# Mixture-of-experts kernel on one core: TensorE's order written out, and three groups of transfers moved to another queue

## The chip, the core and the metric

The kernel runs on one core of a Trainium2 chip. The metric is the device time of one execution in microseconds; lower is better. The engines are named as in the profile: PE (TensorE), DVE (VectorE), ACT (ScalarE), POOL (GpSimd) and SP (SyncE, which here only issues transfers). Each of these engines runs its own instructions in a fixed order, and an instruction that waits holds up all behind it on its engine.

## What is computed

Two transformer blocks are applied to 256 tokens of width 1024, in float32. The first block has attention, then a mixture of experts, then a gated side input; the second has attention beside a gated recurrence, then a feed-forward part. The change touches only the mixture of experts:

```python
logits = xt @ w_router + b_router            # 256 tokens, 32 experts
top_logit, top_e = top_k(logits, 4)
gate = softmax(top_logit)
# for each expert e and the tokens xs that chose it
hh = xs @ w_gu[e] + b_gu[e]                  # 1024 -> 2048
glu, lin = split(hh)
act = min(glu, 7) * sigmoid(1.702 * min(glu, 7)) * (clip(lin, -7, 7) + 1)
y = act @ w_dn[e] + b_dn[e]                  # 1024 -> 1024
out[token] += gate * y
```

## The kernel before

All weights are read once from HBM. Each expert has 12 MiB of them: four chunks of 2 MiB of `w_gu`, keys `("gu", e, 0..3)`, and two chunks of 2 MiB of `w_dn`, keys `("dn", e, 0..1)`. A list `plan` holds all chunks in the order in which they are wanted: for each e the four gu chunks of expert e and then the two dn chunks of expert e-1. `load_next(ring)` takes the next entry of the plan and starts its transfer into a buffer of one of four rings (a: 3 buffers, b: 5, c: 1, d: 1, the last until expert 10 alone). `done(key)` is called behind the last matmul on a chunk and starts the next chunk into the freed buffer, so a transfer waits until PE has finished with the buffer. Ring a takes none of the last six expert chunks; it is kept for `("pg", 0)`, `("pg", 1)` and `("in2", 0)`, the first weights of the next stage. The chunk `("R",)`, a table for the second block, comes in between at expert 16.

Nearly all chunks are issued by SP. Two of the last four, `("dn", 30, 1)` and `("dn", 31, 0)`, are issued by POOL, and the last, `("dn", 31, 1)`, is issued by SP in two halves.

At most 64 tokens of an expert are handled by the main loop. The steps for one expert, with their names and lines:

- `slots(e)`: DVE builds two one-hot matrices from the token positions, `oh` and `gg`.
- `gather(e)` (L949 to L961): 48 small bf16 matmuls pick the expert's tokens into `xg` (PSUM), which DVE multiplies into SBUF; then two transposes and four tiny matmuls turn `gg` and the gates into the tile `y`, which DVE copies into `gt` and `gs`.
- `up(e)` (L973): 64 matmuls on the four gu chunks; two ACTIVATEs evict the result into `h1`.
- `glu(e)` (L988): eight transposes of `h1`, then the clamped activation on DVE and ACT, giving `gl`.
- `down_part(e, c)` (L1009): 16 matmuls on a dn chunk, twice; then ACT and DVE evict `y` into a high part (`li`) and a low part (`sg`).
- `scatter(e)` (L1037): 16 matmuls spread the rows of `y` over the tokens, and DVE adds them onto `h`.

The order of the calls in the loop is that in the diff below. It is not the order on the engines: a scheduler of the language, working from its own estimates, orders each engine's instructions, and `tc.issue_after` ties some of them. With `tc.manual_schedule(engines={PE})` PE's instructions keep the order in which the program calls them, and the other engines stay with the scheduler.

Tokens past an expert's 64 are handled by `past_slots()`, once, at expert 14. It is a branch on the largest count (`tc.If`, L1075 and L1076), with loops, matmuls and transfers in it. The inputs do not take it, but every engine has to pass it.

The functions with their lines:

Of the kernel before, what the change touches and what calls it, by code (L numbers as in the profile page):

```python
# [25 lines left out]
FT = mybir.dt.float32  # L26
# [5 lines left out]
OP = mybir.AluOpType  # L32
# [4 lines left out]
P = 128  # L37
S = 256
D = 1024
E = 32  # L40
# [64 lines left out]
def block_kernel(ctx: ExitStack, tc: tile.TileContext, A, out, dbg=None, parts=("t1", "moe", "over", "t3")):  # L105
    nc = tc.nc
    V, SC, PE, G, SY = nc.vector, nc.scalar, nc.tensor, nc.gpsimd, nc.sync
# [15 lines left out]
    def tt(o, a, b, op):  # L123
        return V.tensor_tensor(out=o, in0=a, in1=b, op=op)  # L124
# [20 lines left out]
    xn = keep.tile([P, 2, D], FT, name="h")  # L145
# [37 lines left out]
    wg, wd = A["w_gu"], A["w_dn"]  # L183
# [27 lines left out]
    def load_next(ring):  # L211
        i = state["next"]
        if i >= len(plan) or (ring != "a" and i >= stop_moe) or (ring == "d" and not state["d"]):
            return
        if ring == "a" and stop_moe - 6 <= i < stop_moe:

            state["held"] += 1
            return
        state["next"] = i + 1
        key, ap, shape = plan[i]  # L220
        t = rings[ring].tile([P, 4096], FT, name="w")
        n = int(np.prod(shape[1:]))
        v = t[:, :n]
        if len(ap.shape) == 3:
            v = v.rearrange("p (a b) -> p a b", b=ap.shape[2])
        if i == 0:
            for h in range(2):
                SY.dma_start(v[:, h], ap[:, h])
        elif key in (("dn", E - 2, 1), ("dn", E - 1, 0)):
            G.dma_start(v, ap)  # L230
        elif key == ("dn", E - 1, 1):
            for h in range(2):
                SY.dma_start(v[:, 2 * h:2 * h + 2], ap[:, 2 * h:2 * h + 2])
        else:
            SY.dma_start(v, ap)
        if key == ("R",):
            SY.dma_start(t[0:E, 3072:3072 + D], A["b_dn"])
        live[key] = (t, ring)
        if i + 1 == stop_moe:
            for _ in range(state["held"]):  # L240
                load_next("a")
# [648 lines left out]
    sl_ = {}  # L890
# [49 lines left out]
    xgs, GTs, GSs, ysb = {}, {}, {}, {}  # L940

    def gather(e):
        oh, gg = sl_.pop(e)
        px = px_.tile([P, 8, CAP], FT, name="xg")
        for kd in range(8):
            n = 0
            for t in range(2):
                for i in range(3):
                    PE.matmul(px[:, kd], u3[i][:, t, kd * P:(kd + 1) * P], oh[:, t], start=(n == 0), stop=(n == 5))  # L949
                    n += 1  # L950
        xg = mw.tile([P, 8, CAP], FT, name="xg", bufs=1)
        tt(xg, px, vec[:, VCOL["g_moe"]:VCOL["g_moe"] + 8].unsqueeze(2).to_broadcast([P, 8, CAP]), OP.mult)
        pgt = py_.tile([P, 512], FT, name="y")
        for t in range(2):
            PE.transpose(pgt[:, t * P:(t + 1) * P], gg[:, t], ident)
        for t in range(2):
            PE.matmul(pgt[:, S:S + 2], gg[:, t], gtab[:, t, e], start=(t == 0), stop=(t == 1))
        gt = mw.tile([P, S], FR, name="gt", bufs=3)
        V.tensor_copy(gt, pgt[:, 0:S])
        gs = mw.tile([P, 2], FT, name="gs", bufs=3)  # L960
        V.tensor_copy(gs, pgt[:, S:S + 2])  # L961
        xgs[e], GTs[e], GSs[e] = xg, gt, gs

    def up(e, aside=None):
        xg = xgs.pop(e)
        ps = pg_.tile([P, 2, 512], FT, name="gu")
        for c in range(4):
            w = W(("gu", e, c)).rearrange("p (k n) -> p k n", k=2)
            for kk in range(2):
                k = 2 * c + kk  # L970
                for n in range(2):
                    for s in range(2):
                        PE.matmul(ps[64 * s:64 * s + 64, n], xg[:, k],  # L973
                                  w[:, kk, s * 1024 + n * 512:s * 1024 + (n + 1) * 512],
                                  start=(k == 0), stop=(k == 7))
            done(("gu", e, c))
            if aside and c == 0:
                aside()
        h1 = mw.tile([P, 2, 512], FT, name="h1", bufs=1)
        for n in range(2):  # L980
            act(h1[:, n], ps[:, n], AF.Copy, scale=GSs[e][:, 1:2])
        return h1
# [39 lines left out]
            ysb[e] = hi, lo  # L1022
        return i

    def down(e, aT):
        for c in range(2):
            i = down_part(e, aT, c)
        return i

    def scatter(e):  # L1030
        y, gt = ysb.pop(e), GTs.pop(e)
        for t in range(2):
            pp = [pc_.tile([P, 512], FT, name="sc") for _ in range(2)]
            for s in range(2):
                sl = slice(64 * s, 64 * s + 64)
                for i in range(2):
                    PE.matmul(pp[s], gt[sl, t * P:(t + 1) * P], y[i][sl], start=(i == 0), stop=(i == 1))  # L1037
            for s in range(2):
                hs = xn[:, t, s * 512:(s + 1) * 512]
                held["xn"] = tt(hs, pp[s], hs, OP.add)  # L1040

    def bias_dn(home):
        bdn = W(("R",))[0:E, 3072:3072 + D]
# [24 lines left out]
    def past_slots():  # L1068
# [7 lines left out]
        with tc.If(mv > CAP):  # L1076
            for t in range(2):
                ts(rb, ones, rh[:, t:t + 1], None, OP.mult)
                PE.matmul(pacc[:, 0:P], rb, ident, start=True, stop=True)
                V.tensor_copy(rBo, pacc[:, 0:P])  # L1080
                for k in range(8):
                    for i in range(3):
                        PE.matmul(pacc[:, 0:P], u3[i][:, t, k * P:(k + 1) * P], identb, start=(i == 0), stop=(i == 2))
                    stt(uT[:, k], pacc[:, 0:P], vc("g_moe", k), rBo, OP.mult, OP.mult)
                with tc.For_i(0, E, 1) as e:
                    cv = nc.values_load(cnti[0:1, ds(e, 1)], min_val=0, max_val=S)
                    with tc.If(cv > CAP):
                        V.tensor_copy(gc, gover[:, t, ds(e, 1)])
                        V.tensor_copy(bg, bgu[:, ds(e, 1), :].rearrange("p o n -> p (o n)"))
                        for m in range(8):  # L1090
                            for s in range(2):
                                for c in range(4):
                                    SY.dma_start(w[:, 2 * c:2 * c + 2],
                                                 wg[ds(e, 1), c, :, :, s * 1024 + m * P:s * 1024 + (m + 1) * P]
                                                 .rearrange("o p k n -> p (o k) n"))
                                for k in range(8):
                                    PE.matmul(pacc[:, s * P:(s + 1) * P], w[:, k], uT[:, k], start=(k == 0), stop=(k == 7))
                            ts(gl, pacc[:, 0:P], bg[:, m:m + 1], 7.0, OP.add, OP.min)
                            act(sg, gl, AF.Sigmoid, scale=1.702)
                            ts(li, pacc[:, P:2 * P], bg[:, 8 + m:9 + m], 7.0, OP.add, OP.min)  # L1100
                            ts(li, li, -7.0, 1.0, OP.max, OP.add)
                            tt(gl, gl, sg, OP.mult)
                            tt(aT[:, m], gl, li, OP.mult)
                        for s in range(8):
                            for c in range(2):
                                SY.dma_start(w[:, 4 * c:4 * c + 4], wd[ds(e, 1), c, :, :, s * P:(s + 1) * P]
                                             .rearrange("o p k n -> p (o k) n"))
                            for k in range(8):
                                PE.matmul(pacc[:, 0:P], aT[:, k], w[:, k], start=(k == 0), stop=(k == 7))
                            hs = xn[:, t, s * P:(s + 1) * P]  # L1110
                            stt(hs, pacc[:, 0:P], gc, hs, OP.mult, OP.add)

    gather(0)
    slots(1)
    h1 = up(0, lambda: gather(1))
    aT = glu(0, h1)
    for e in range(E - 1):
        h1 = up(e + 1, (lambda: scatter(E - 3)) if e == E - 2 else None)
        if e == E - 2:
            break  # L1120
        if e > 0:
            scatter(e - 1)
        if e + 2 < E:
            slots(e + 2)
        aN = glu(e + 1, h1)
        down(e, aT)
        aT = aN
        if e + 2 < E:
            gather(e + 2)
        if e == E_OVER - 4:  # L1130
            state["d"] = False
        if e == E_OVER and "over" in parts:
            past_slots()
        if e == E_REL:
            bias_dn(rel_flip())
    i = down_part(E - 2, aT, 0)
    with tc.issue_after(i.ins):
        aL = glu(E - 1, h1)
# [594 lines left out]
```

## Time and profile before

| | |
|---|---|
| time, median of 3 runs | 1438.92 us (1438.46 to 1439.38) |
| time of the profiled execution | 1439.79 us, of which the span is 1438.0 us |
| PE busy | 1341.6 us, 93% |
| DVE, ACT, POOL busy | 44%, 26%, 3% |
| moved by DMA | 482.39 MB, 335 GB/s over the span |
| mean granted clock of PE | 0.98 of full speed |

The span runs from the first to the last instruction that was profiled. The mixture of experts takes some 930 us of it, from 166 us (first matmul of `up(0)`) to 1094 us (last matmul of `down_part(31, 1)`). Before it lie the first block's projections and attention; behind it the rest of the first block and the whole second block.

### The profile page before, as it was taken

How to read it: one execution, taken by the hardware profiler on the slowest of the kernel's cores; microseconds unless marked ns; L12 is line 12 of the kernel's file. 1: busy time of each engine (PE TensorE's matmuls, PEld its weight loads, DVE VectorE, ACT ScalarE, POOL GpSimd, SP SyncE). 2: the span in 40 equal slices, each digit the busy share in tenths (PEclk: the TensorE clock that was granted, in tenths of full speed). 3: DMA queues.
4: the chain of work that ended last, by engine and by line, in shares of the span. 5: the costliest groups of instructions: out<-in, count | busy, mean ns of one | idle time of the engine just before them, and what ended most of it. 6: DMA issues, size and time to landing. Idle time of an engine off the chain costs nothing. (4 is left out here: it accounts for less than half of the span.)

```text
span 1438.0 us, 19752 instructions
## 1 busy us (share of the span) xinstructions
PE 1341.6 (93%) x8361; PEld 748.1 (52%) x8362; DVE 637.1 (44%) x1250; ACT 370.5 (26%) x639; POOL 39.8 (3%) x55
## 2 busy tenths in 40 slices
PE   6999999999999999989999999999988999999997
PEld 6877533433333333333333333333325887899997
DVE  5676522323223322314323232323225878677776
ACT  5555210100011001001001000100014647565554
POOL 1010200000000000000000000000000101000000
PEclk9999999999999999999999999999999999999999
DMA  7338899999999999989999999999996543345540
GB/s 280 111 135 366 332 427 428 426 427 427 427 426 426 428 427 427 427 348 428 427 427 427 427 425 429 427 426 427 427 425 254 173 149 132 132 180 199 202 152 30
DMA packets 40656, 482.39 MB, mean 335 GB/s; under 512 B 4105, under 2 KB 4641, under 8 KB 12657
## 3 DMA queue, kind: packets, MB, share of 16 engines
q1 hardware_dynamic: 38656, 473.39, 79.4%
q0 software_dynamic: 1040, 6.55, 1.2%
q10 hardware_dynamic: 864, 1.13, 0.3%
q8 instruction: 67, 1.10, 0.3%
q14 instruction: 29, 0.23, 0.0%
HBM read 479.99 MB, written 1.06 MB: 335 GB/s over the span
## 5 line engine op out<-in xcount | busy, mean ns | idle before, releaser
L973 PE MATMUL gu<-w,xg 128*64 128x512 f32 x2048 | 475.4, 617 | 3.4 <-DMA w<-w_gu 3.1
L973 PEld LDWEIGHTS gu<-w,xg 128*64 128x64 f32 x2048 | 146.1, 141 | 294.4 <-issue 288.3
L1009 PE MATMUL y<-w,gl 128*64 128x512 f32 x1024 | 235.3, 598 | 2.9 <-DVE sg L127 1.6
L121 ACT ACTIVATE h<-gu,gs 128x512 f32<-128x512 f32 x64 | 40.5, 683 | 548.5 <-PE gu L973 548.5
L259 DVE TENSOR_TENSOR wl<-w,wh 128x1024 fp32r<-128x1024 f32 (+2 forms) x124 | 148.2, 1206 | 47.1 <-ACT wh L121 46.5
L121 ACT ACTIVATE wh<-w 128x1024 fp32r<-128x1024 f32 (+2 forms) x125 | 128.3, 1038 | 96.4 <-PE acc L277 21.7
L124 DVE TENSOR_TENSOR h<-sc,h 128x512 f32<-128x512 f32 x126 | 81.7, 687 | 125.7 <-PE sc L1037 123.4
L124 DVE TENSOR_TENSOR xg<-xg,vec 128x512 f32<-128x512 f32 x32 | 22.1, 691 | 255.3 <-PE gu L973 254.5
L1009 PEld LDWEIGHTS y<-w,gl 128*64 128x64 f32 x1024 | 68.7, 136 | 121.2 <-issue 115.7
L276 PE MATMUL wk<-ul,wh 128*128 128x256 f32 x336 | 94.5, 281 | 0.2 <-DVE ul L124 0.2
L275 PE MATMUL wk<-uh,wh 128*128 128x256 f32 x336 | 94.5, 281 | 0.0
L277 PE MATMUL wk<-uh,wl 128*128 128x256 f32 x336 | 94.3, 281 | 0.0
L127 DVE SCALAR_TENSOR_TENSOR sg<-y,gs,li 128x512 fp32r<-128x512 f32 x31 | 23.3, 751 | 115.9 <-ACT li L121 115.7
L949 PEld LDWEIGHTS <-u 128*128 128x128 bf16 x1536 | 54.2, 98 | 28.9 <-issue 28.3
L121 ACT ACTIVATE li<-y,gs 128x512 fp32r<-128x512 f32 x31 | 21.3, 687 | 181.6 <-PE y L1009 179.5
L276 PEld LDWEIGHTS wk<-ul,wh 128*128 128x128 f32 x336 | 63.4, 189 | 1.2 <-DVE ul L124 0.4
L275 PEld LDWEIGHTS wk<-uh,wh 128*128 128x128 f32 x336 | 63.3, 188 | 1.0 <-ACT uh L121 0.2
L277 PEld LDWEIGHTS wk<-uh,wl 128*128 128x128 f32 x336 | 63.4, 189 | 0.0
L949 PE MATMUL xg<-oh,u 128*128 128x64 bf16 x1536 | 59.8, 193 | 0.7 <-ACT proj L121 0.7
L988 PE MATMUL tr<-cf,h 128*128 128x128 f32 x256 | 39.2, 286 | 22.7 <-ACT h L121 22.6
L124 DVE TENSOR_TENSOR gl<-tr,bgu 128x512 f32<-128x512 f32 x32 | 22.1, 692 | 76.5 <-PE tr L988 76.5
L988 PEld LDWEIGHTS tr<-cf,h 128*128 128x128 f32 x256 | 27.0, 140 | 50.7 <-ACT h L121 48.2
(411 smaller groups left out, 1752.0 us busy)
## 6 DMA issues: line engine op xcount, KB each, us to landing
w<-w_gu SPq DMA_DIRECT2D x128, 2048.0 KB, 22.3
w<-w_dn SPq DMA_DIRECT2D x61, 2048.0 KB, 20.8
w<-w_up SPq DMA_DIRECT2D x11, 2048.0 KB, 8.0
w<-w_in SPq DMA_DIRECT2D x7, 2048.0 KB, 10.1
w<-w_down SPq DMA_DIRECT2D x5, 2048.0 KB, 7.5
w<-w_o SPq DMA_DIRECT2D x4, 2048.0 KB, 8.5
w<-w_dn POOLq DMA_DIRECT2D x2, 2048.0 KB, 17.9
w<-w_pg SPq DMA_DIRECT2D x2, 2048.0 KB, 27.4
```

The costliest lines, as they stand in the source:

```text
L121: return SC.activation(out=o, in_=i, func=f, **kw)
L124: return V.tensor_tensor(out=o, in0=a, in1=b, op=op)
L127: return V.scalar_tensor_tensor(out=o, in0=a, scalar=s, in1=b, op0=op0, op1=op1)
L259: eng.tensor_tensor(out=lo, in0=src, in1=hi.bitcast(FT), op=OP.subtract)
L275: PE.matmul(o, l[0], r[0], start=first, stop=False)
L276: PE.matmul(o, l[0], r[1], start=False, stop=False)
L277: PE.matmul(o, l[1], r[0], start=False, stop=last)
L949: PE.matmul(px[:, kd], u3[i][:, t, kd * P:(kd + 1) * P], oh[:, t], start=(n == 0), stop=(n == 5))
L973: PE.matmul(ps[64 * s:64 * s + 64, n], xg[:, k], w[:, kk, s * 1024 + n * 512:s * 1024 + (n + 1) * 512], start=(k == 0), stop=(k == 7))
L988: PE.transpose(pt[:, m], hf[:, m * P:(m + 1) * P], ident)
L1009: i = PE.matmul(ps[64 * s:64 * s + 64], aT[:, k], w[:, kk, s * 512:(s + 1) * 512], start=(k == 0), stop=(k == 7))
```

## The change

Three things are changed. PE's instructions from the first `gather` to the end of the expert loop stay in the order of the program, and that order is written anew: `gather` gives its second half to a function `gates_of`, which runs inside `up` behind the third chunk; `scatter` is cut in two, behind the first and second chunk of the next `up`; `glu`'s transposes and the next `gather` stand between the two parts of `down`. The transfers inside the branch `past_slots` are issued by POOL instead of SP. The chunks `("dn", 30, 1)` and `("dn", 31, 0)` are issued by SP instead of POOL.

```diff
         if i == 0:
             for h in range(2):
                 SY.dma_start(v[:, h], ap[:, h])
-        elif key in (("dn", E - 2, 1), ("dn", E - 1, 0)):
-            G.dma_start(v, ap)
         elif key == ("dn", E - 1, 1):
...
     def gather(e):
-        oh, gg = sl_.pop(e)
+        oh = sl_[e][0]
...
         tt(xg, px, vec[:, VCOL["g_moe"]:VCOL["g_moe"] + 8].unsqueeze(2).to_broadcast([P, 8, CAP]), OP.mult)
+        xgs[e] = xg
+
+    def gates_of(e):
+        gg = sl_[e][1]
         pgt = py_.tile([P, 512], FT, name="y")
...
-        xgs[e], GTs[e], GSs[e] = xg, gt, gs
-    def up(e, aside=None):
+        GTs[e], GSs[e] = gt, gs
+    def up(e, aside):
...
             done(("gu", e, c))
-            if aside and c == 0:
-                aside()
+            if c in aside:
+                aside[c]()
...
-    def scatter(e):
-        y, gt = ysb.pop(e), GTs.pop(e)
-        for t in range(2):
-            pp = [pc_.tile([P, 512], FT, name="sc") for _ in range(2)]
+    def scatter(e, t):
+        y, gt = ysb[e], GTs[e]
...
-                                    SY.dma_start(w[:, 2 * c:2 * c + 2],
+                                    G.dma_start(w[:, 2 * c:2 * c + 2],
...
-                                SY.dma_start(w[:, 4 * c:4 * c + 4], wd[ds(e, 1), c, :, :, s * P:(s + 1) * P]
+                                G.dma_start(w[:, 4 * c:4 * c + 4], wd[ds(e, 1), c, :, :, s * P:(s + 1) * P]
...
+    order = ExitStack()
+    order.enter_context(tc.manual_schedule(engines={mybir.EngineType.PE}))
     gather(0)
     slots(1)
-    h1 = up(0, lambda: gather(1))
+    h1 = up(0, {0: lambda: gates_of(0), 2: lambda: gates_of(1)})
+    gather(1)
     aT = glu(0, h1)
     for e in range(E - 1):
-        h1 = up(e + 1, (lambda: scatter(E - 3)) if e == E - 2 else None)
+        aside = {}
+        if e + 2 < E:
+            slots(e + 2)
+            aside[2] = lambda: gates_of(e + 2)
+        if e > 0:
+            aside[0] = lambda: scatter(e - 1, 0)
+            aside[1] = lambda: scatter(e - 1, 1)
+        h1 = up(e + 1, aside)
         if e == E - 2:
             break
-        if e > 0:
-            scatter(e - 1)
-        if e + 2 < E:
-            slots(e + 2)
+        down_part(e, aT, 0)
         aN = glu(e + 1, h1)
-        down(e, aT)
+        gather(e + 2)
+        down_part(e, aT, 1)
         aT = aN
-        if e + 2 < E:
-            gather(e + 2)
         if e == E_OVER - 4:
...
+    order.close()
     i = down_part(E - 2, aT, 0)
```

## Rows read from the trace of the kernel before

**Rows 1.** Page, part 2: rate of all transfers in 40 slices of the span.
```profile
GB/s 280 111 135 366 332 427 428 426 427 427 427 426 426 428 427 427 427 348 428 427 427 427 427 425 429 427 426 427 427 425 254 173 149 132 132 180 199 202 152 30
```

**Rows 2.** Windows: length, busy us (instructions) by engine, PE's clock, DMA share, GB/s.
```profile
186.00:630.00 444.00, 418.14 (x2585) 163.47 (x2582) 128.78 (x272) 40.19 (x63) 0.00 (x0) 0.98 1.00 425
652.00:1082.00 430.00, 398.91 (x2364) 154.00 (x2365) 125.46 (x258) 39.68 (x62) 1.14 (x2) 0.98 1.01 427
428.87:457.01 28.14, 26.23 (x166) 10.36 (x167) 8.60 (x18) 2.58 (x5) 0.00 (x0) 1.00 1.01 427
```

**Rows 3.** Timeline of PE, one expert: start, us, instruction, [idle before <-releaser].
```profile
428.87 0.65 PE L988 MATMUL tr<-cf,h 128*128 128x128 f32 x4 [0.84 <-ACT h L121]
...
439.48 0.50 PE L1037 MATMUL sc<-li,gt 64*128 64x512 f32 x2 [0.79 <-ACT li L121]
...
441.40 3.65 PE L973 MATMUL gu<-w,xg 128*64 128x512 f32 x16
```

**Rows 4.** Waits of PE, 166 to 1060 us: total us, times, longest.
```profile
PE tr L988 <- ACT h L121: 22.6, 27, 0.8
PE sc L1037 <- ACT li L121: 19.7, 25, 0.8
PE y L955 <- DVE sg L127: 8.9, 27, 1.6
```

**Rows 5.** Chunks issued by SP at 180 to 260 and 1000 to 1012 us.
```profile
DMA to landing us min/median/max: 12.3/17.4/20.6
...
DMA to landing us min/median/max: 28.2/28.5/28.9
```

**Rows 6.** The branch's line: ns min/median/max, first and last start us.
```profile
L1076 SPq EVENT_SEMAPHORE  x9: 17/17/17, 619.4 to 633.4; - x9
L1076 ACTq EVENT_SEMAPHORE  x2: 17/17/17, 630.3 to 630.4; - x2
...
L1076 POOLq COMPARE_BRANCH  x1: 45/45/45, 163.2 to 163.2; - x1
```

**Rows 7.** Windows around SP's passing of the branch, columns as in rows 2.
```profile
624.00:632.00 8.00, 7.16 (x62) 3.45 (x60) 1.66 (x3) 1.26 (x2) 0.00 (x0) 1.00 0.77 326
632.00:642.00 10.00, 10.00 (x62) 3.41 (x58) 0.57 (x3) 0.00 (x0) 0.00 (x0) 1.00 0.74 278
```

**Rows 8.** Timeline of PE, the first expert.
```profile
169.49 1.57 PE L949 MATMUL xg<-oh,u 128*128 128x64 bf16 x48
...
171.59 10.52 PE L973 MATMUL gu<-w,xg 128*64 128x512 f32 x48
```

**Rows 9.** Window in the first expert, columns as in rows 2.
```profile
170.00:180.00 10.00, 10.00 (x83) 4.50 (x81) 1.30 (x6) 0.00 (x0) 0.00 (x0) 1.00 0.95 339
```

**Rows 10.** Issues at 1022.2, 1042.5, 1061.5 us: KB, us to landing.
```profile
w<-w_gu SPq DMA_DIRECT2D x1, 2048.0 KB, 36.4
...
w<-w_dn POOLq DMA_DIRECT2D x1, 2048.0 KB, 14.2
...
w<-w_dn SPq DMA_DIRECT2D x1, 1024.0 KB, 20.5
```

**Rows 11.** Timeline of PE, the last expert.
```profile
1057.45 3.65 PE L973 MATMUL gu<-w,xg 128*64 128x512 f32 x16
...
1077.14 3.65 PE L1009 MATMUL y<-w,gl 128*64 128x512 f32 x16 [1.35 <-DMA w<-w_dn]
1080.73 1.09 PE L988 MATMUL tr<-cf,h 128*128 128x128 f32 x8
...
1086.98 7.09 PE L1009 MATMUL y<-w,gl 128*64 128x512 f32 x32 [1.57 <-DVE sg L127]
```

**Rows 12.** Windows for PE's clock, columns as in rows 2.
```profile
457.01:485.20 28.19, 27.11 (x164) 10.76 (x166) 7.91 (x17) 1.84 (x3) 0.00 (x0) 0.94 1.01 427
...
1060.00:1080.00 20.00, 15.51 (x72) 4.88 (x70) 1.29 (x2) 1.26 (x2) 0.00 (x0) 1.00 1.00 419
...
1098.00:1105.00 7.00, 6.22 (x23) 5.64 (x24) 6.49 (x9) 4.30 (x6) 0.00 (x0) 0.51 0.00 1
```

More of the change, by code (lines that the diff above doesn't have):

```diff
@@ L1023, in down_part @@
         return i
[L1025 to L1028, printed above, removed]
-    def scatter(e):
-        y, gt = ysb.pop(e), GTs.pop(e)
-        for t in range(2):
-            pp = [pc_.tile([P, 512], FT, name="sc") for _ in range(2)]
+    def scatter(e, t):
+        y, gt = ysb[e], GTs[e]
+        if t == 1:
+            del ysb[e], GTs[e]
+        pp = [pc_.tile([P, 512], FT, name="sc") for _ in range(2)]
+        for i in range(2):
             for s in range(2):
                 sl = slice(64 * s, 64 * s + 64)
[L1036 to L1040, printed above, removed]
+                PE.matmul(pp[s], gt[sl, t * P:(t + 1) * P], y[i][sl], start=(i == 0), stop=(i == 1))
+        for s in range(2):
+            hs = xn[:, t, s * 512:(s + 1) * 512]
+            held["xn"] = tt(hs, pp[s], hs, OP.add)
     def bias_dn(home):
```

## The prediction

> **What bounds the kernel now.** I read the 40 slices first. From the sixth slice on, for some 900 us, the transfer rate stands at 427 GB/s and hardly moves [rows 1]; over two long windows it is 425 and 427 with a DMA share of 1.00 and more [rows 2]. So the transfers of the expert weights run back to back at a rate that nothing here exceeds: 2 MiB at 427 GB/s is 4.91 us a chunk, 29.5 us for an expert of six chunks. The dents are what can be won there; slice 18 (348) is the largest.
>
> Then PE. One expert without a fall of the clock takes it 28.14 us, 26.23 busy [rows 2]. The 1.91 us between are three waits: 0.84 before the transposes for `h1`'s eviction and 0.79 before the scatter for `y`'s [rows 3], and 0.28 (8.9 over 27) for `y`'s low part [rows 4]. Rows 4 hold PE's three largest waits between 166 and 1060 us, 51.2 us in all. None of them is for a chunk. So PE is not starved, though the transfers are at their limit. That fits together because data are ahead: at 180 to 260 us a chunk lands 17.4 us after its issue [rows 5]; with ten buffers cycled in 49.1 us, the other 31.7 us pass between landing and freeing. At 1000 to 1012 us it is 28.5 us [rows 5], with nine buffers 44.2 - 28.5 = 15.7 us. PE with its clock falls needs nearly what the transfers need and eats up that lead slowly.
>
> Last I read the end. The last half chunk is issued at 1061.5 and lands 20.5 us later, at 1082.0 [rows 10]. PE's last `down` matmul ends at 1086.98 + 7.09 = 1094.07 [rows 11], 12.1 us behind the data. What follows (scatter, the next stage) hangs on PE.
>
> **The change part by part.**
>
> *PE's order.* No PE instruction is added. `h1`'s eviction gets the first `down` chunk as cover, 16 matmuls, which take the 3.65 us of any chunk [rows 11]; `y`'s gets the first gu chunk, 3.65 us [rows 3], against waits of 0.84, 0.79 and 0.28. DVE's multiply into `xg` gets the second `down` chunk. All three waits should go: 26.2 us an expert at full clock. The window means 0.98 [rows 2] say that some 4% of the time is at the lower level; I keep that, 0.02 x 29 = 0.6 us an expert, so 26.8. The hand-set order makes PE wait in place where the scheduler filled in; queued behind a late `xg` are the next 64 matmuls, and the buffers and so SP wait for those. The bounds of this part are 0 and 1.9 us of waits coming back per expert; I take 0, since DVE is busy 8.60 of 28.14 us and ACT 2.58 [rows 2].
>
> By itself this wins almost nothing: at 26.8 against 29.5 us PE gains 2.7 us an expert on the data, the lead of some 28 us (31.7 less the 4 us in which a chunk is in use) is gone after ten to fifteen experts, and from then on PE waits for chunks. The waits on evictions become waits on transfers. The value is that at the end PE stands right at the data.
>
> In the first expert the transfers are not yet saturated: 339 GB/s in 170 to 180 us [rows 9] is (427 - 339)/427 x 10 = 2.1 us lost. `gather(1)`, 1.57 us, stands between chunks 0 and 1 of `up(0)` and holds back the freeing of chunk 1 [rows 8]; it goes behind chunk 3, while `gates_of(0)` takes the place of `gates_of(1)`. Bounds 0 and 2.1; I take **1.6**, the gather's own time.
>
> *The branch.* SP's nine semaphore steps on skipping it run from 619.4 to 633.4 us; ACT, which issues no transfer there, has two, 0.1 us apart [rows 6]. SP waits until its own transfers in flight have landed. With it the stream dries up: 326 GB/s over 8 us and 278 over 10 us [rows 7] cost 1.9 + 3.5 = 5.4 us of transfer time. With POOL as issuer SP has no transfer in the branch and only passes it; PE's pause there stays, and the queue of issued chunks covers it. POOL takes its branch at 163.2 us [rows 6] with no chunk in flight, and what comes behind on its queue is wanted only near the end: cost nothing, and if POOL paused for as long as SP did, still nothing. The gain lies between 0 (SP still stopped) and 5.4; I take **5.4**, since the rows tie the stop to the issuer.
>
> *The last chunks.* A gu chunk issued by SP at 1022.2 lands after 36.4 us, at 1058.6; a dn chunk issued by POOL 20.3 us later lands after 14.2 us, at 1056.7 [rows 10]. So POOL's two chunks, wanted after gu(31), overtake gu(31, 1) to gu(31, 3), and PE waits for what was pushed back: 1.35 us before `down_part(30, 0)` [rows 11], with the glu of expert 31 and 7.09 us of `down` still to come. In one queue the chunks land in the order of use, at 4.91 us. Counted back from the last landing L: gu(31, 3) at L - 19.6, PE done with it at L - 16.0; dn(30, 0) lands at L - 14.7 and is done by L - 11.1; eight transposes, 1.09 us [rows 11], to L - 10; dn(30, 1) lands at L - 9.8, done by L - 6.2; `y`'s eviction ends at about L - 4.6 (wait of 1.57 now [rows 11]); dn(31, 0) lands at L - 4.9, done by L - 1; the last quarter of the 7.09 us, 1.8, follows L. PE ends 1.8 instead of 12.1 us behind the data: **10.3 us**. The lower bound is 0 (the first rival). The buffer of the first came free at 1042.5, and SP's next issue is about 19 us later [rows 10], so on SP's queue the two hold up nothing. The first weights of the next stage now land some 5 us after L; they must be split before PE uses them about 8 us after its last expert matmul. That is close, 0 to 1.5 us, taken as 0.
>
> *Sum.* 1.6 + 5.4 + 10.3 = 17.3 us. Against its own time, 1439.79 - 17.3 = 1422.5; that execution is 0.87 us above the median of the runs, so 1421.6, rounded to **1422**.
>
> **Rivals.** *The two chunks' queue is worth nothing*: the same DMA engines serve both queues, L stays, and if PE's end hangs on L by other work, only 1.6 + 5.4 remain: 1432. Against it stands the overtaking in rows 10. The Trainium skill (DMA: Bandwidth & Descriptors, section Issuing engines are not separate DMA queues) says that transfers started by different engines interleave on the same DMA engines, so that several issuers save only issue time; by that this edit gives nothing. The trace agrees on the interleaving, 1056.7 before 1058.6, and that is just what changes the order.
>
> *PE stays behind the data*: the waits come back elsewhere, 1.9 us an expert. PE then keeps its 28.8 us mean (from its first matmul at 166 us to gu(31) at 1057.45 [rows 11], over 31 experts), reaches gu(31) as late as now, and saves only the waits of the last expert, some 5 us: 1434. It decides from about 1.4 us of new waits an expert; under that the lead is still used up.
>
> *The branch still stops SP*, because the language ties every engine to it: 1422 + 5.4 = 1427. ACT's two steps speak against it.
>
> *Slower: PE's clock.* PE now waits at nearly every chunk, in gaps of up to 1.3 us (4.91 between landings less 3.65 of matmuls). Today an expert with a fall has mean clock 0.94, 12% at 1.2 instead of 2.4 GHz, 1.7 us lost [rows 12]. If the new gaps hold PE at 1.2 GHz for more than 5.2 us an expert, the loss is over 28.8 - 26.2 = 2.6 us and PE is slower than now; at 7 us it is 29.7 us an expert, 0.9 x 31 = 28 us more, less the 5 us at the end: 1461. Against it: from 1060 to 1080 us PE waited three times for chunks, was busy 15.5 of 20 us, and was granted 1.00 [rows 12]; and a slower PE no longer waits. The Trainium skill (TensorE: Matmul & The Clock Gate, section HAM oscillation — how this bites in real kernels) tells of a kernel whose short groups of matmuls between waits for DMA threw the clock back every time; by it this rival would be the likely one, which no row here shows.
>
> **How the numbers follow.** Forecast 0.72; SP still stopped 0.08; PE behind 0.08; queue worth nothing 0.06; clock 0.04; hardly any change for a reason I don't see, 0.02. The forecast's own range: the stretch at half clock behind the experts (0.51 over 7 us [rows 12], 3.4 us lost) can vanish or double, the first expert gives 0 to 2.1, the last quarter may run at half clock (1.8), the next stage's first split may be 1.5 late: 1417.5 to about 1428. To leave out no more than 2 in 10 I go to 1430, which takes in the stopped SP. Changes under 0.2% (2.9 us) count as none, about what a measurement of this kernel can tell. All cases but the clock and the last are faster by more: 0.94; slower 0.035; same 0.025.
>
> **What would show it.** Right: PE's waits on ACT and DVE at L988 and L1037 gone, waits for DMA at L973 and L1009 from the middle experts on; no dent near 630 us, SP's steps at L1076 down to two or three; every chunk of the end landing in order 4.9 us apart; PE's last L1009 matmul under 3 us behind the last landing. Wrong: PE's mean clock well under 0.98 between 600 and 1050 us, time to landing still near 28 us instead of about 40 at the end, new waits on DVE's `xg`, or a pause in the stream at the branch.

## The result, and the profile after

The changed kernel takes 1426.09 us (median of 4 runs, 1424.20 to 1427.41) against 1438.69 (4 runs, 1437.98 to 1439.38) for the kernel before: ratio 0.9909, interval 0.9898 to 0.9921. It is 12.6 us faster where 17 were forecast, and the time lies in the range. Its profiled execution took 1425.2 us with a span of 1423.4; PE's mean granted clock was 0.993 instead of 0.980.

Page of the changed kernel, parts 2 and 4: rate of all transfers in 40 slices, and shares of the chain that ended last.

```profile
GB/s 283 112 106 375 324 420 427 427 427 426 425 428 427 428 426 425 427 413 426 427 428 427 427 427 427 427 426 426 428 426 350 192 126 134 135 195 198 198 148 30
...
DMA 47%; PE 46%; DVE 4%; ACT 1%; issue 1%; POOL 1%; DVEq 0%; SPq 0%; ACTq 0%; POOLq 0%
```

Slice 18, which held the largest dent (348 in [rows 1]), now shows 413. The transfers are nearly half of the chain that ended last.

Windows of the changed kernel, columns as in rows 2.

```profile
170.00:180.00 10.00, 10.00 (x54) 4.03 (x52) 1.00 (x5) 0.00 (x0) 0.00 (x0) 1.00 0.88 323
186.00:600.00 414.00, 387.54 (x2482) 153.55 (x2478) 125.11 (x272) 39.39 (x62) 0.00 (x0) 1.00 1.01 427
600.00:660.00 60.00, 54.80 (x330) 21.74 (x332) 15.83 (x35) 4.48 (x7) 0.00 (x0) 0.94 1.01 419
620.00:640.00 20.00, 16.21 (x114) 6.73 (x112) 6.12 (x12) 1.32 (x2) 0.00 (x0) 0.91 1.00 410
660.00:1080.00 420.00, 378.87 (x2312) 147.48 (x2310) 117.76 (x247) 39.21 (x61) 0.00 (x0) 1.00 1.01 426
1085.00:1100.00 15.00, 12.67 (x66) 10.38 (x64) 13.72 (x18) 12.93 (x20) 1.09 (x2) 1.00 0.75 288
```

The two long stretches run at 427 and 426 GB/s with PE's clock at 1.00, where the kernel before had 0.98 [rows 2]. From 620 to 640 us, where the dent was, the rate is 410 at a DMA share of 1.00; [rows 7] have 326 and 278 at shares of 0.77 and 0.74. Behind the experts (1085 to 1100) the clock is 1.00, where rows 12 have 0.51 over 7 us.

PE's waits in the changed kernel, 160 to 1060 us, answering to rows 4.

```profile
PE gu L978 <- DMA w<-w_gu: 36.9, 58, 3.8
PE y L1014 <- DMA w<-w_dn: 25.3, 19, 1.4
PE gu L978 <- PEq L1077: 4.1, 1, 4.1
```

The largest waits of before, 51.2 us on ACT and DVE, are gone; their place is taken by 62.2 us on chunks. That is more waiting, and the kernel is faster: PE now stands at the data. Up to 398 us there is no wait for a chunk; from there, in expert 9, they stand in every expert but 16, 18 and 19, near the branch and the table `("R",)`.

The branch's line in the changed kernel, columns as in rows 6.

```profile
L1077 POOLq EVENT_SEMAPHORE  x5: 17/43/43, 171.7 to 172.0; - x5
...
L1077 PEldq COMPARE_BRANCH  x1: 6419/6419/6419, 593.2 to 593.2; - x1
...
L1077 SPq EVENT_SEMAPHORE  x1: 17/17/17, 602.2 to 602.2; - x1
```

SP has one semaphore step instead of nine [rows 6]. The steps are now POOL's, five within 0.3 us at 172. PE's queue needs 6.4 us for its own branch, of which 4.1 us are the third wait above.

What the nine steps waited for can be read in the kernel before. SP's last chunk ahead of the branch, issued at 612.7 us, has this row (columns as in rows 10):

```profile
w<-w_gu SPq DMA_DIRECT2D x1, 2048.0 KB, 20.4
```

It lands at 633.1, and a step of SP starts at 633.1; the chunk before it and the table land at 628.2 and 623.0, and steps start at 628.2 and 623.0. So SP did stand until its own transfers had landed.

Issues of the changed kernel at 1000 to 1012 and at 1050 us (the last half chunk), columns as in rows 5 and 10.

```profile
DMA to landing us min/median/max: 39.1/39.1/39.1
...
w<-w_dn SPq DMA_DIRECT2D x1, 1024.0 KB, 30.6
```

A chunk lands 39.1 us after its issue, where it was 28.5 [rows 5]: the queue of issued chunks is ten microseconds longer. The last half chunk, issued at 1050.0, lands at 1080.6; before it landed at 1082.0 [rows 10].

Timeline of PE in the changed kernel: first chunk, last expert, and what follows it.

```profile
167.75 3.65 PE L978 MATMUL gu<-w,xg 128*64 128x512 f32 x16 [0.85 <-DVE xg L124]
...
1050.74 3.65 PE L978 MATMUL gu<-w,xg 128*64 128x512 f32 x16 [0.49 <-DMA w<-w_gu]
...
1060.93 3.65 PE L978 MATMUL gu<-w,xg 128*64 128x512 f32 x16 [1.26 <-DMA w<-w_gu]
1065.93 3.65 PE L1014 MATMUL y<-w,gl 128*64 128x512 f32 x16 [1.35 <-DMA w<-w_dn]
1069.52 1.09 PE L993 MATMUL tr<-cf,h 128*128 128x128 f32 x8
1070.76 3.65 PE L1014 MATMUL y<-w,gl 128*64 128x512 f32 x16
1075.98 7.09 PE L1014 MATMUL y<-w,gl 128*64 128x512 f32 x32 [1.57 <-DVE sg L127]
...
1087.77 1.97 PE L1280 MATMUL wk<-cf,h 128*128 128x128 f32 x16 [2.33 <-DVE h L124]
```

From the second chunk of expert 31 (1050.74) to `down_part(30, 1)` (1070.76) four steps take 20.0 us, 5.0 each, the rate of the transfers. `down_part(31, .)` ends at 1075.98 + 7.09 = 1083.1, 2.5 us behind the last landing.

So the two profiled executions, 14.6 us apart, are taken apart in three pieces. The last landing came 1.4 us earlier (1082.0 to 1080.6). PE's end behind it shrank from 12.1 to 2.5, which is 9.6. From there to the end of the span it took 1423.4 - 1083.1 = 340.3 instead of 1438.0 - 1094.1 = 343.9, which is 3.6. That last piece is partly luck: the other ten profiles of this document need 340.7 to 342.8 us there, so the two that are compared here are the extremes. The medians lie 12.6 us apart.

### The profile page after: what moved, and what is told of

Read it like the earlier page. It is cut to its first block, busy times and chain, and to the rows that moved or that the text cites. A ratio compares the mean times of both kernels' runs of the same rounds, so it can differ in the third digit from the quotient of the medians.

```text
span 1423.4 us, 19768 instructions
## 1 busy us (share of the span) xinstructions
PE 1315.6 (92%) x8361; PEld 741.2 (52%) x8362; DVE 627.9 (44%) x1250; ACT 370.3 (26%) x639; POOL 38.9 (3%) x53
## 4 chain that ended last, share of the span: by engine, by line
DMA 47%; PE 46%; DVE 4%; ACT 1%; issue 1%; POOL 1%; DVEq 0%; SPq 0%; ACTq 0%; POOLq 0%
DMA w<-w_gu 27%; DMA w<-w_dn 19%; PE gu L978 9%; PE y L1014 5%; PE acc L273 3%; PE acc L274 3%; PE acc L275 3%; PE wk L274 3%; PE wk L275 3%; PE wk L273 3%; PE pj L273 2%; PE pj L275 2%; PE pj L274 2%; PE xg L948 1%; PE tr L993 1%
## 5 line engine op out<-in xcount | busy, mean ns | idle before, releaser
L978 PEld LDWEIGHTS gu<-w,xg 128*64 128x64 f32 x2048 | 142.0, 137 | 315.9 <-issue 248.9
L1014 PEld LDWEIGHTS y<-w,gl 128*64 128x64 f32 x1024 | 72.9, 136 | 161.1 <-issue 156.4
L121 ACT ACTIVATE sg<-gl 128x512 f32<-128x512 f32 x32 | 20.1, 630 | 182.8 <-DVE gl L131 176.1
L963 DVE CAST gt<-y 128x256 fp32r<-128x256 f32 x32 | 13.6, 424 | 112.8 <-PE y L961 112.8
L948 PE MATMUL xg<-oh,u 128*128 128x64 bf16 x1536 | 50.0, 193 | 0.7 <-ACT proj L121 0.7
L948 PEld LDWEIGHTS <-u 128*128 128x128 bf16 x1536 | 49.1, 98 | 2.6 <-issue 2.3
L127 DVE SCALAR_TENSOR_TENSOR cv<-wk,vec,cv 128x255 f32<-128x255 f32 x88 | 42.2, 480 | 8.7 <-ACT cv L121 7.1
## 6 DMA issues: line engine op xcount, KB each, us to landing
w<-w_gu SPq DMA_DIRECT2D x128, 2048.0 KB, 39.1
w<-w_dn SPq DMA_DIRECT2D x63, 2048.0 KB, 39.1
w<-w_in SPq DMA_DIRECT2D x7, 2048.0 KB, 10.5
```

Source lines behind the costliest of these rows:

```text
L121: return SC.activation(out=o, in_=i, func=f, **kw)
L127: return V.scalar_tensor_tensor(out=o, in0=a, scalar=s, in1=b, op0=op0, op1=op1)
L978: PE.matmul(ps[64 * s:64 * s + 64, n], xg[:, k], w[:, kk, s * 1024 + n * 512:s * 1024 + (n + 1) * 512], start=(k == 0), stop=(k == 7))
L1014: i = PE.matmul(ps[64 * s:64 * s + 64], aT[:, k], w[:, kk, s * 512:(s + 1) * 512], start=(k == 0), stop=(k == 7))
```

## The experiments

Each was timed beside the kernel before, whose medians were 1437.79 to 1439.17 us in these experiments, so kernels are compared by their ratios. "Landing" is the last chunk's, and "lag" is the time from it to the end of PE's last `down` matmul.

| kernel | PE's order | branch on POOL | last chunks on SP | time, us | ratio and interval | landing, us | lag, us |
|---|---|---|---|---|---|---|---|
| before | | | | 1438.69 | 1 | 1082.0 | 12.1 |
| e1_order | yes | | | 1438.67 | 0.9999, 0.9990 to 1.0008 | 1082.8 | 12.1 |
| e2_branch | | yes | | 1436.35 | 0.9977, 0.9968 to 0.9987 | 1079.3 | 12.1 |
| e3_last | | | yes | 1434.37 | 0.9964, 0.9951 to 0.9977 | 1082.3 | 7.7 |
| e4_queues | | yes | yes | 1434.56 | 0.9958, 0.9943 to 0.9974 | 1079.0 | 11.3 |
| e5_order_branch | yes | yes | | 1436.45 | 0.9982, 0.9970 to 0.9994 | 1080.5 | 12.1 |
| e6_order_last | yes | | yes | 1429.74 | 0.9943, 0.9926 to 0.9959 | 1083.1 | 2.5 |
| changed kernel | yes | yes | yes | 1426.09 | 0.9909, 0.9898 to 0.9921 | 1080.6 | 2.5 |

Landing and lag are those of each kernel's profiled execution. The gains don't add: the three parts alone give 0.1, 3.3 and 5.2 us by their ratios, 8.6 together, and the whole change gives 13.1 by its ratio.

**PE's order alone** (e1_order). Against the changed kernel:

```diff
+        elif key in (("dn", E - 2, 1), ("dn", E - 1, 0)):
+            G.dma_start(v, ap)
...
-                                    G.dma_start(w[:, 2 * c:2 * c + 2],
+                                    SY.dma_start(w[:, 2 * c:2 * c + 2],
...
-                                G.dma_start(w[:, 4 * c:4 * c + 4], wd[ds(e, 1), c, :, :, s * P:(s + 1) * P]
+                                SY.dma_start(w[:, 4 * c:4 * c + 4], wd[ds(e, 1), c, :, :, s * P:(s + 1) * P]
```

> The kernel before with PE's new order alone: the branch's transfers stay on SP and the two late chunks on POOL. Theory A (at the end PE hangs on the landing of the chunks, and the parts only pay together): the pause of the stream at the branch stays, 5.2 us, and the POOL chunks still overtake, so PE's last down matmul stays about 12 us behind the last landing; only the first expert (about 1 us) and the clock behind the experts (0 to 3.6 us) can gain: 1434 to 1438 us. Theory B (covering the evictions is the gain, 1.9 us in each of 31 experts): at most 1428 us.

Measured: 1438.67 us over 11 runs, ratio 0.9999. PE's two largest waits from 160 to 1060 us:

```profile
PE gu L980 <- DMA w<-w_gu: 39.9, 61, 4.1
PE y L1016 <- DMA w<-w_dn: 29.4, 21, 3.2
```

Its timeline of the last expert:

```profile
1072.97 3.65 PE L980 MATMUL gu<-w,xg 128*64 128x512 f32 x16 [0.86 <-DMA w<-w_gu]
1077.99 3.65 PE L1016 MATMUL y<-w,gl 128*64 128x512 f32 x16 [1.36 <-DMA w<-w_dn]
```

The 51.2 us of waits on evictions became 69.3 us of waits on chunks, at no gain. `down_part(30, 0)` starts at 1077.99 behind a wait for its chunk, as at 1077.14 in [rows 11]: this PE is ready, and what it needs lands late.

**The branch's transfers alone** (e2_branch). Against the kernel before:

```diff
-                                    SY.dma_start(w[:, 2 * c:2 * c + 2],
+                                    G.dma_start(w[:, 2 * c:2 * c + 2],
...
-                                SY.dma_start(w[:, 4 * c:4 * c + 4], wd[ds(e, 1), c, :, :, s * P:(s + 1) * P]
+                                G.dma_start(w[:, 4 * c:4 * c + 4], wd[ds(e, 1), c, :, :, s * P:(s + 1) * P]
```

> The kernel before with the branch's transfers on POOL alone. Theory A: no pause of the stream near 630 us, SP has two or three semaphore steps at the branch instead of nine, all chunks after it land about 5 us earlier; PE, with its old order, is behind the data and saves no more than its waits for chunks in the last expert: 1433 to 1437 us. Theory C (SP stops at the branch whoever issues its transfers): 1438 to 1439 us.

Measured: 1436.35 us, ratio 0.9977: 3.3 us, interval 1.9 to 4.6. Window of this kernel at the branch:

```profile
630.00:640.00 10.00, 9.75 (x90) 4.82 (x92) 1.69 (x5) 0.77 (x2) 0.00 (x0) 1.00 1.00 426
```

The dent is gone, so the stop belonged to the issuer of the branch's transfers. The landing moved by 2.7 us, where some 5 were expected; the lag did not move.

**The last chunks alone** (e3_last). Against the kernel before:

```diff
-        elif key in (("dn", E - 2, 1), ("dn", E - 1, 0)):
-            G.dma_start(v, ap)
```

> The kernel before with the two late chunks on SP alone. Theory A: the last landing stays near 1082 us, the gu chunks of the last expert land 5 to 9 us earlier and PE no longer waits for them, but with its old order it comes to them late (near 1057 us), so it saves only its waits there, some 4.5 us: 1433 to 1436 us. Theory D (all queues share the same DMA engines, so the issuer does not matter): 1438 to 1439 us.

Measured: 1434.37 us, ratio 0.9964: 5.2 us. Timeline of PE, last expert:

```profile
1058.50 3.65 PE L971 MATMUL gu<-w,xg 128*64 128x512 f32 x16
1062.74 10.52 PE L971 MATMUL gu<-w,xg 128*64 128x512 f32 x48
...
1082.88 7.09 PE L1007 MATMUL y<-w,gl 128*64 128x512 f32 x32 [1.57 <-DVE sg L127]
```

PE reaches expert 31 as late as before (1057.45 in [rows 11]) and then finds all its chunks there: 48 matmuls run without a break. Now PE is what is late, and the lag is 7.7 us of PE's own work. The lateness of the chunks and that of PE lay side by side, so taking away one of them gives half.

**Both moves of queues, in the old order** (e4_queues). The two edits above together.

> The kernel before with both moves of transfers, PE's order as before. Theory A: data are 5 us earlier still, but PE is the last, so this is no better than either move alone: 1433 to 1436 us, PE's last down matmul some 12 us behind the last landing. Theory E (each part has its own gain and they add): 1428 to 1430 us.

Measured: 1434.56 us, ratio 0.9958, no better than e3_last; that the gains would add to 1428 to 1430 falls. PE's two largest waits from 160 to 1060 us:

```profile
PE tr L986 <- ACT h L121: 22.6, 27, 0.8
PE sc L1035 <- ACT li L121: 19.7, 25, 0.8
```

The landing came at 1079.0, 3.3 us earlier than in e3_last, and the lag grew by 3.6 to 11.3: PE sets the end here, still held up by evictions, and a stream that is done sooner buys nothing. Two of the eight executions took 1427.84 and 1429.73 us, with a mean granted clock of 0.985 where the other six had 0.978 to 0.982; that is in keeping with PE being the one that is late.

**Order and branch** (e5_order_branch). The changed kernel with the two chunks back on POOL:

```diff
+        elif key in (("dn", E - 2, 1), ("dn", E - 1, 0)):
+            G.dma_start(v, ap)
```

> The changed kernel with the two late chunks back on POOL: PE's order and the branch's transfers, without the last part. Theory A (at the end PE hangs on the landing, and the chunks' order of landing sets how far behind it ends): the last landing about 5 us earlier than before, PE's last down matmul 12 us behind it as before: 1431 to 1435 us. Theory F (the order alone lets PE end at the data once the branch no longer stops the stream): 1425 to 1428 us.

Measured: 1436.45 us, ratio 0.9982, 1.5 us above the upper end of what theory A gave; the landing came 1.5 us earlier than in the kernel before, where about 5 were expected. Timeline of PE, last expert:

```profile
1070.64 3.65 PE L980 MATMUL gu<-w,xg 128*64 128x512 f32 x16 [1.25 <-DMA w<-w_gu]
1075.64 3.65 PE L1016 MATMUL y<-w,gl 128*64 128x512 f32 x16 [1.34 <-DMA w<-w_dn]
...
1085.48 7.09 PE L1016 MATMUL y<-w,gl 128*64 128x512 f32 x32 [1.57 <-DVE sg L127]
```

PE waits for `gu(31, 3)` until 1070.64, where the changed kernel has it at 1060.93. The same bytes, landing in another order, cost 0.9982 - 0.9909 = 0.0073, 10.5 us. The lag is 12.1 us, as in all four kernels that keep the chunks on POOL: it is the work that is still to come behind the chunk that was pushed back.

**Order and last chunks** (e6_order_last). The changed kernel with the branch back on SP:

```diff
-                                    G.dma_start(w[:, 2 * c:2 * c + 2],
+                                    SY.dma_start(w[:, 2 * c:2 * c + 2],
...
-                                G.dma_start(w[:, 4 * c:4 * c + 4], wd[ds(e, 1), c, :, :, s * P:(s + 1) * P]
+                                SY.dma_start(w[:, 4 * c:4 * c + 4], wd[ds(e, 1), c, :, :, s * P:(s + 1) * P]
```

> The changed kernel with the branch's transfers back on SP: PE's order and the last chunks on SP. Theory A: the pause near 630 us is back and costs its 5.2 us of stream, and PE ends 2.5 us behind the last landing as in the changed kernel: 1429 to 1433 us. Theory G (PE sets the pace, so that the stream's pause is hidden): 1425 to 1428 us.

Measured: 1429.74 us, ratio 0.9943, within what theory A gave. Windows of this kernel at the branch:

```profile
625.00:635.00 10.00, 7.44 (x36) 2.48 (x34) 3.45 (x7) 0.69 (x1) 0.00 (x0) 1.00 0.57 241
635.00:645.00 10.00, 5.78 (x24) 1.79 (x22) 1.36 (x3) 0.00 (x0) 0.00 (x0) 0.82 0.93 359
```

The dent is back, the lag stays at 2.5, the landing is at 1083.1.

**Evictions uncovered again** (e7_uncovered). The changed kernel with `glu`'s transposes ahead of the first `down` chunk:

```diff
-        down_part(e, aT, 0)
         aN = glu(e + 1, h1)
+        down_part(e, aT, 0)
         gather(e + 2)
```

> The changed kernel with the transposes of glu moved ahead of the first down chunk, so that PE stands idle some 0.8 us for h1's eviction in each of 30 experts. Theory A (the stream sets the pace, PE has nearly 3 us to spare per expert): the idle time comes out of the waits for chunks, 1424 to 1428 us. Theory B (covering the evictions is the gain): 0.8 x 30 = 24 us lost, about 1450 us.

Measured: 1425.73 us, ratio 0.9912, the changed kernel's time. PE's waits from 160 to 1060 us:

```profile
PE gu L978 <- DMA w<-w_gu: 30.4, 51, 2.1
PE tr L993 <- ACT h L121: 25.4, 30, 0.9
...
PE y L1014 <- DMA w<-w_dn: 0.3, 1, 0.3
```

25.4 us of waits on `h1`'s eviction return, and the waits for `down` chunks fall from 25.3 to 0.3: they are paid out of the time that PE would wait for data anyway. This cover is not what made the change pay; an order with 0.85 us of such waits an expert, where the old one had 1.9, also gets PE to the data before the end. Which of the other moves in PE's order it takes for that was not tried.

**The table for `ple_proj` later** (e8_pp_late). In the changed kernel the chunk `("pp",)` and the 16 matmuls on it move from ahead of the experts into expert 22:

```diff
-    want(("pp",), A["w_pp"].rearrange("(k p) n -> p k n", p=P), [P, 2, 1024])
...
+        if e == E_PP:
+            want(("pp",), A["w_pp"].rearrange("(k p) n -> p k n", p=P), [P, 2, 1024])
...
-                pp = z_tile()
+                pp = pc_.tile([P, 512], FT, name="sc")
...
-    with tc.issue_after(lmm.ins):
-        ple_proj()
...
+        if e == E_PP:
+            ple_proj()
```

> The changed kernel with the chunk w_pp and its product with p moved from ahead of the experts into expert 22, in PSUM buffers of the scatter. Ahead of the experts it held a ring buffer until about 164 us and left the stream idle; in the loop PE has time to spare. Theory A (every us of stream regained before the experts is a us of the total): the idle stretches of the stream between 147 and 186 us shrink by 3 to 5 us, less nothing for the chunk itself, which is moved and not added, less 2.5 us because its transfer now falls into the full stream: 1422 to 1426 us. Rival (the first experts are paced by PE, so that nothing is regained): 1426 to 1429 us.

Measured: 1429.72 us, ratio 0.9935, interval 0.9921 to 0.9950: slower than the changed kernel, and above both ranges. Timeline of PE ahead of the first expert:

```profile
161.12 0.21 PE L857 MATMUL tp<-selb,upperb 128*128 128x32 bf16 x1 [5.16 <-DVE selb L855]
...
164.30 2.72 PE L948 MATMUL xg<-oh,u 128*128 128x64 bf16 x48 [2.86 <-DVE oh L132]
...
167.81 5.71 PE L978 MATMUL gu<-w,xg 128*64 128x512 f32 x16 [0.78 <-DVE xg L125]
```

Windows of this kernel, and behind them the first of the two in the changed kernel:

```profile
160.00:170.00 10.00, 5.23 (x59) 3.56 (x61) 7.91 (x31) 1.71 (x6) 2.26 (x2) 0.50 0.51 216
170.00:180.00 10.00, 10.00 (x46) 3.51 (x44) 0.88 (x4) 0.00 (x0) 0.00 (x0) 0.90 0.56 198
...
160.00:170.00 10.00, 7.90 (x73) 3.83 (x75) 7.28 (x29) 3.75 (x10) 2.27 (x2) 1.00 0.89 333
```

The moved matmuls had filled the time in which PE waits for DVE's routing work. Without them PE stood idle for 5.16 and 2.86 us, the clock over 160 to 170 us was 0.50 of full speed, the 1.2 GHz level, where the changed kernel has 1.00, and the first chunk took 5.71 instead of 3.65 us. The first buffers came free later, and the stream ran at 198 GB/s where the changed kernel has 323. The landing came at 1085.2, 4.6 us later, of which the moved chunk's own 1 MiB, now in the full stream, is 1.05 MB at 427 GB/s, 2.5 us. What looked like a delay ahead of the experts had kept the clock up.

**Work to hold the clock behind the experts** (e9_filler), and **the changed kernel once more** (e10_again), timed together. The filler is ten matmuls behind the last scatter whose result nobody reads:

```diff
+    idle = pg_.tile([P, 2, 512], FT, name="gu")
+    with tc.issue_after(lpo.ins):
+        for _ in range(10):
+            PE.matmul(idle[:, 0], identb, u3[0][:, 0, 0:512], start=True, stop=True)
```

> The changed kernel with ten matmuls added whose result nobody reads, behind the last scatter and ahead of the next stage's transposes, where PE stands idle 2.3 us. Theory H (the idle time there is what throws PE's clock to 1.2 GHz in some executions, which costs the next stage 1.7 to 3.5 us): no stretch at 0.5 within 15 us behind the experts, the rest of the span from PE's last down matmul near 340 us each time, median 1423 to 1425.5 us. Rival (the clock falls for what lies before, or the fillers only delay the transposes): same as the changed kernel, 1425.5 to 1428 us.

> The changed kernel once more, on the same chip as the one with the fillers: 1424 to 1428 us by every theory.

Measured: 1425.29 us (0.9911, 0.9896 to 0.9926) with the filler and 1425.99 (0.9913, 0.9900 to 0.9927) without. Window behind the experts, with the filler:

```profile
1085.00:1100.00 15.00, 14.81 (x76) 11.07 (x75) 13.31 (x18) 12.93 (x20) 1.69 (x3) 1.00 0.75 283
```

The same window of the changed kernel's second profile:

```profile
1085.00:1100.00 15.00, 14.01 (x63) 12.11 (x64) 12.83 (x16) 12.52 (x20) 1.11 (x2) 0.89 0.74 285
```

The filler's clock is 1.00 and the plain kernel's 0.89, in the first profile 1.00: in this stretch the same kernel gets either. The medians differ by 0.7 us, less than the intervals can tell, so the filler's worth is not shown. Nor was the rest of the span near 340 us, as theory H expected: it took 342.0 us with the filler. Its clock fell further on, here beside the changed kernel's first profile:

```profile
1209.00:1215.00 6.00, 5.22 (x12) 4.12 (x13) 4.45 (x4) 2.63 (x3) 0.00 (x0) 0.50 0.17 33
...
1209.00:1215.00 6.00, 5.95 (x20) 4.82 (x21) 3.72 (x4) 2.01 (x3) 0.00 (x0) 0.74 0.26 55
```

The second profile of the changed kernel needed 342.1 us from PE's last `down` matmul to the end of the span, where the first needed 340.3, yet has the same span, 1423.4: its landing was at 1078.8 and its experts began at 166.4.

## Why the prediction was right, and what of it was mis-sized

**Bound and mechanism: right.** The transfers' rate was the limit and PE had a lead of data to use up. e1_order shows both: 69 us of waits on chunks appear, and the time stays. In the changed kernel the first such wait comes at 398 us, behind nine experts, where "ten to fifteen experts" were forecast: from expert 2 (209.85 us) to expert 9 (389.47) PE took 25.7 us an expert, not 26.8.

**PE's order: right** in "by itself this wins almost nothing": forecast 0 apart from the first expert, measured 0.1 us, interval -1.2 to 1.4. It is the condition for the rest: with it the two moves of queues give 0.9999 - 0.9909 = 0.0090, 13.0 us, without it (e4_queues) 6.0. The kept allowance for falls of the clock, 0.6 us an expert, was not needed (1.00 in both long stretches). The cover for `h1`'s eviction, a term of the 26.2 us, could be left out (e7_uncovered).

**First expert, 1.6 us: not found.** e1_order has this edit too, and its landing is 0.8 us later than before's, of which 0.4 is a later start (166.3 instead of 165.9). In the changed kernel 170 to 180 us ran at 323 GB/s against 339 [rows 9], with experts that began 1.85 us later (167.75). The gather was in the way, as [rows 8] show, but freeing that chunk sooner moved nothing at the end. A gain of under 1 us could be hidden in the spread of these starts.

**The branch, 5.4 us: the mechanism right, the term too large.** The step failed in taking the whole dent as gain. SP's steps are gone and so is the dent (e2_branch, and back in e6_order_last), but by itself the move gave 3.3 us, interval 1.9 to 4.6. On top of the other two it gave 0.9943 - 0.9909 = 0.0034, 4.9 us, uncertain by some 2.9. The mean landing of the four kernels with the branch on SP is 1082.55, of the other four in the table and e7_uncovered (1080.0) 1079.9: 2.7 us. The chunks tell where the rest went. From the landing of `("gu", 16, 2)` to that of `("gu", 18, 2)`, around the branch, the four take 68.5 to 68.8 us, and the seven profiles with the branch on POOL (e8_pp_late left out) 63.7 to 64.6: 4.6 us in the mean. The DMA shares of [rows 7] give nearly that, 0.23 x 8 + 0.26 x 10 = 4.4, where their rates gave 5.4. The 419 GB/s over 60 us in the changed kernel are no remainder of the stop: their DMA share is 1.01, and the kernel before has 412 at 1.01 from 610 to 620 us, ahead of its stop. The other 1.9 us are lost elsewhere. In the seven, `("gu", 16, 2)` lands 0.8 us later in the mean, and PE's first chunk began at 166.0 to 168.2 against 165.9 to 166.3 in the four, 0.9 us later; and from `("gu", 18, 2)` to the last landing they take 410.2 to 411.3 us against 409.4 to 409.8, 1.1 us more. Neither has a cause that a run shows. In the two latest starts of the seven the clock fell near 75 us; POOL's five steps at the branch come behind the start (171.7 against 167.75), which speaks against POOL as the cause of it.

**The last chunks, 10.3 us: right.** The lag went from 12.1 to 2.5 us, 9.6. In time it is worth 10.5 us with the branch moved (changed kernel against e5_order_branch) and 0.9999 - 0.9943 = 0.0056, 8.1 us, without it. The missing 0.7 is in the last step: `y`'s eviction does end at L - 4.6, as reckoned (1080.6 - 1075.98), but from there the 7.09 us run through without a break and end at L + 2.5. "The last quarter of the 7.09 us, 1.8, follows L" took PE to be waiting for the last half chunk, which it never did.

Put together, 0 + 3.3 + 9.6 = 12.9 us, and 12.6 were measured by the medians, 13.1 by the ratio. That they meet so closely is partly luck: the 3.3 are uncertain by 1.4, the 9.6 are a lag in two profiles, and the clock behind the experts is left out.

**The clock behind the experts.** The forecast kept the stretch at 0.51 and let it "vanish or double". In the profiled execution it vanished, 3.6 us, and by luck stood in for most of the 5.6 us that the landing fell short of its 7.0; in the second profile part of it is there. Two kernels with the same end agree: e6_order_last has 1.00 from 1083 to 1098 us and takes 340.7 us from PE's last `down` matmul on, e7_uncovered 0.89 and 342.6.

**The rivals.** PE behind the data, with 1434, is just what e3_last and e4_queues measured (1434.4 and 1434.6): the rival's price was right, and PE's order is what turned it away. Its threshold of 1.4 us of new waits an expert was not reached: e7_uncovered brings back 0.85 and loses nothing. SP still stopped, forecast at 1427 for a sum with all terms full, falls by its one semaphore step.

The queue worth nothing falls by e5_order_branch. The Trainium skill (DMA: Bandwidth & Descriptors, section Issuing engines are not separate DMA queues) holds that several issuers only save issue time. The runs differ: the same two chunks from POOL instead of SP cost 8.1 and 10.5 us, through the order of landing.

The clock rival falls too: PE waited for chunks 77 times up to 1060 us and was granted 1.00 in both long stretches. The Trainium skill (TensorE: Matmul & The Clock Gate, section HAM oscillation — how this bites in real kernels) tells of groups of matmuls between DMA waits that lose the clock every time. The prediction took that to make this rival the likely one, but that section's kernel waits some 3 to 5 us each time. Here groups of 3.65 us with waits of mostly 0.5 to 1.4 us kept it, while e8_pp_late, with 5.16 us of idle time ahead of short matmuls, did lose it.

## What to carry to other kernels

Where a stream of weights sets the time, look at the end of the stream: what PE still has to do when the last bytes land is paid in full, and a second queue that lets late chunks overtake earlier ones lengthens it. Two things that are late side by side (PE and the chunks here) each look worth half or nothing alone, so they are tried together before either is dropped. A branch that is never taken can still stop an engine whose queue would issue transfers in it, as SP here stood until its last chunk had landed; give those to an engine that has none in flight.

## What was not expected of the hardware

PE was granted more clock when it waited more: 0.98 in the two long stretches of the kernel before [rows 2], busy 94% and 93% of them, and 1.00 in those of the changed one, busy 94% and 90%, in spite of its 77 waits for chunks. No run here tells why. Passing the branch took PE's own queue 6.4 us (one instruction of 6419 ns at 593.2; 6212 ns in the kernel before), of which 4.1 us became a wait; the stream ran on through it, at 424 GB/s from 590 to 610 us. And the same kernel began its experts at 166.4 in one execution and 167.75 in another, as much as the smaller terms here are worth, so that no single profile settles them.
